# The last FFN block's down-projection as seven block products, and the delayed norm's stores issued one step later

## The chip, the cores and the metric

The kernel runs on one core of a Trainium2 chip. The metric is the device time of one execution in microseconds (us), the median of repeated runs. In this text PE is TensorE's matmul, PEld its weight load, DVE is VectorE, ACT is ScalarE, POOL is GpSimd, and SP is SyncE, whose queue (SPq in the profile) issues the DMAs this text is about.

## The reference, cut to what matters

One layer of a hybrid encoder: RMSNorm, a combined projection, chunk-band attention beside an mLSTM, an output projection, and then a gated convolutional feed-forward network. The change touches only the last part:

```python
def conv_ffn(h, buf, w_up, w_conv, b_conv, w_down):
    u = h @ w_up
    ext = jnp.concatenate([buf.astype(u.dtype), u], axis=1)
    y = b_conv
    for j in range(CONV_W):
        y = y + ext[:, j:j + S] * w_conv[j]
    gate, up = jnp.split(y, 2, axis=-1)
    out = (jax.nn.gelu(gate, approximate=True) * up) @ w_down
    return out, ext[:, S:]
...
    ffn, new_buf = conv_ffn(rms_norm(x, norm_g[2]), conv_buf, w_up, w_conv, b_conv, w_down)
    x = x + rms_norm(ffn, norm_g[3])
```

D_MODEL is 1024, D_FF is 2816, and there are 2048 prompt tokens and 8 x 16 sample tokens, so 17 token tiles of 128. `@ w_down` has 2816 = 22 x 128 rows of contraction and 1024 = 2 x 512 output columns. All is float32.

## The kernel before, in words

**Precision.** Each float32 operand is split into a high part (ACT casts it to the matmul's format) and a low part (DVE subtracts the high part); a product is three matmuls, hi·hi, hi·lo and lo·hi (`mm3`, lines 95 to 97). So every weight block of 128 x 512 costs one ACT cast (line 1259) and one DVE subtraction (line 1260) before PE may use it, and every piece of the gated activations costs the same.

**The feed-forward part** works on three blocks of token tiles, `FBLOCKS`: block 0 has tiles 0 to 5, block 1 has tiles 6 to 11, and block 2, the last, has tiles 12 to 15 and the sample tile 16, which is five tiles. For each block an *up* phase runs over 22 values of f: seven block products instead of eight (Strassen-Winograd; P1 to P7), the convolution on DVE, ACT and POOL, the gate (`gt`), and a store of it to DRAM. Then comes the *down* phase, which loads the gated activations back and multiplies them by `w_down`.

**Down, plain form (blocks 0 and 2 before).** Two halves of the output columns (`dh`), and in each 22 steps k; a step is 3 matmuls of 512 columns for each token tile. Weight blocks come four at a time (`load_w`, tiles `wdr` from DRAM, `wdh`/`wdl` after the split, two buffers of four blocks), activations one k at a time (`fetch`, line 1510, tiles `gr`; `gh`/`gl` after the split). In block 0, `load_down` also forms sums of weight blocks and stores them to `wtd`, for later use. In block 2's second half (`tail`), the last six k are done tile by tile, and after each tile `finish` does its norm at once: the sum of squares on ACT, the reciprocal root on POOL (lines 78 and 84), two scalings on DVE (line 1410), the additions of x on POOL and DVE (line 1412), two stores (line 1413).

**Down, seven products (block 1 before).** The up phase stores, besides the gated activations, four sums of their blocks (`gs`, line 1611) to `gsd`. The two halves of the token tiles and the two halves of k form a 2 x 2 block product, done as seven products D1, D6, D2, D7, D5, D4, D3. Each has six *units* u: two k each, the last one k. A unit of three tiles is 768 columns (`fetch_unit`, line 1534, tiles `gq`). Each product needs its own 11 weight blocks, from `w_down` or from the sums in `wtd`. When a product ends, its three accumulators are copied or added on (`x2`, `x3`).

**The delayed norm.** Blocks 0 and 1 don't finish their tiles at once. They store both halves of the result to DRAM (`f0d`, `f1d`), and the next block's down phase does the rest of them, as units of the pipe `ahead`, one step after each k or unit: `later` (line 1415) loads the half row `f` and the half of `x` (lines 1419 and 1420), and a step later scales on DVE (line 1422), adds x on POOL (line 1423), and stores on SP (line 1424). That is 12 such half rows for each of blocks 1 and 2.

**What sets the order.** Each engine has a queue worked in order. A scheduler orders the program's instructions by a modelled timeline, except where `keep_in_program_order` fixes one. Almost all DMAs of this part go through SP's queue: one that waits for its data (a store) or for its buffer (a load) holds back all behind it. A DMA also waits for the one eight places before it to land. Buffers: 11 of 128 x 512 (`quad`: raw weights, half rows, x), 4 wide rows (`row`: `gq`, `gr`), 2 + 2 of split weights, 4 of split activations.

## Time and profile before

| | |
|---|---|
| three runs | 2792.59, 2793.82 (median), 2799.96 us |
| the profiled execution | 2789.77 us; its span 2787.7 us |
| block 1: up, and down | about 1850 to 2167 us, and 2167 to 2340 us of the span |
| block 2: up, and down | about 2350 to 2621 us, and 2621 to 2780 us |
| after the last matmul | 2780 to 2787.7 us |

Times in the profile are microseconds from the start of the span. A table of windows has a row for each stretch: its length, the busy time of each engine with the number of instructions in brackets, the clock that PE was granted (1.00 is full), the mean busy share of the 16 DMA engines, and the rate that they moved. A row of a timeline has the start, the length, the engine and line, the operation with the tile that it writes and those that it reads, and in square brackets the idle time before it with what ended that. A wait "<- POOL f L1423" ended with that instruction. Matmuls overlap, so the length of one (some 0.4 us at 512 columns) is not the distance between two.

### The profile page before, as it was taken

To read this page: it belongs to the slowest core of one execution; us is meant where nothing else is said; L and a number is where in the kernel's file an instruction comes from. 1 tells how busy PE (TensorE), PEld (TensorE's weight loads), DVE (VectorE), ACT (ScalarE), POOL (GpSimd) and SP (SyncE) were. 2 spreads that over 40 slices of the span, in tenths; PEclk is the share of its full clock that TensorE was granted. 3 is DMA by queue.
4 is the path that set the end of the run, shared out by engine and by line. 5 is a ranking of instruction groups with operands and counts; after the bars stand their busy time and mean duration, and the time that the engine had idled before them with its cause. 6 is when DMAs were issued, how large, how long until landed. Compare 5 with 4: busy or idle time off the path is not lost.

```text
span 2787.7 us, 47226 instructions
## 1 busy us (share of the span) xinstructions
PE 2711.9 (97%) x16488; PEld 2539.5 (91%) x16488; DVE 1939.6 (70%) x3562; ACT 1421.7 (51%) x2871; POOL 447.3 (16%) x876
## 2 busy tenths in 40 slices
PE   8999999999999999999999999999999899999998
PEld 7899999998899998878999998799999778999987
DVE  5344455655456668756999988658888786888865
ACT  4355455644356666533554455445445565555543
POOL 1000010212000002334211211111111221222221
PEclk9999999999999999999999999999999999999999
DMA  5544355456555455355655449855554797555585
GB/s 185 155 122 133 103 175 162 159 160 213 158 173 147 141 172 182 113 167 176 217 172 176 162 161 324 297 180 167 174 179 165 244 345 230 170 180 179 177 323 192
DMA packets 334316, 516.33 MB, mean 185 GB/s; under 512 B 57122, under 2 KB 162558, under 8 KB 333950
## 3 DMA queue, kind: packets, MB, share of 16 engines
q1 hardware_dynamic: 295486, 479.49, 53.4%
q10 hardware_dynamic: 38592, 33.83, 3.6%
q8 instruction: 129, 2.11, 0.3%
q14 instruction: 109, 0.89, 0.1%
HBM read 371.61 MB, written 144.72 MB: 185 GB/s over the span
## 4 chain that ended last, share of the span: by engine, by line
PE 51%; DVE 4%; DMA 3%; issue 1%; POOL 1%; ACT 1%; SPq 0%; DVEq 0%; POOLq 0%; ACTq 0%
PE uec L95 6%; PE uec L97 6%; PE uec L96 6%; PE dn L97 3%; PE dn L95 3%; PE dn L96 3%; PE ua L97 3%; PE ua L96 3%; PE ua L95 3%; PE dnm L97 2%; PE dnm L95 2%; PE dnm L96 2%; PE wo L95 2%; PE wo L96 2%; PE wo L97 2%; PE ub L96 1%
## 5 line engine op out<-in xcount | busy, mean ns | idle before, releaser
L95 PE MATMUL uec<-B,wuh 128*128 128x384 f32 (+1 forms) x720 | 234.5, 328 | 3.3 <-DVE uu L1466 2.5
L96 PE MATMUL uec<-B,wuh 128*128 128x384 f32 (+1 forms) x720 | 235.1, 327 | 0.0
L97 PE MATMUL uec<-B,wul 128*128 128x384 f32 (+1 forms) x720 | 234.2, 327 | 0.0
L1259 ACT CAST wuh<-wu 128x512 fp32r<-128x512 f32 x255 | 141.7, 617 | 114.5 <-PE uec L96 103.8
L95 PE MATMUL dn<-wdh,gh 128*128 128x512 f32 x444 | 175.1, 394 | 6.1 <-ACT gh L1259 3.4
L96 PE MATMUL dn<-wdl,gh 128*128 128x512 f32 x444 | 175.7, 396 | 0.0
L1260 DVE TENSOR_TENSOR wul<-wu,wuh 128x512 fp32r<-128x512 f32 x255 | 165.3, 684 | 3.5 <-DMA x2d<-mx 3.5
L97 PE MATMUL dn<-wdh,gl 128*128 128x512 f32 x444 | 165.2, 398 | 0.8 <-DVE gl L1260 0.8
L395 DVE CUSTOM_DVE_ANT_0 tmp<-s,nb 128x640 f32<-128x640 f32 (+4 forms) x128 | 94.4, 738 | 96.8 <-PE s L385 95.5
L95 PE MATMUL vo<-wi_h,hT 128*128 128x256 f32 x544 | 155.9, 287 | 0.6 <-DVE mt L201 0.6
L97 PE MATMUL vo<-wi_h,hT 128*128 128x256 f32 x544 | 156.3, 287 | 0.0
L96 PE MATMUL vo<-wi_l,hT 128*128 128x256 f32 x544 | 155.5, 286 | 0.0
L95 PEld LDWEIGHTS uec<-B,wuh 128*128 128x128 f32 x720 | 134.9, 188 | 5.3 <-DVE uu L1466 3.5
L95 PE MATMUL qk<-hT,wi_h 128*128 128x384 f32 (+1 forms) x384 | 129.7, 338 | 7.2 <-ACT qk_st L226 5.9
L96 PEld LDWEIGHTS uec<-B,wuh 128*128 128x128 f32 x720 | 135.3, 188 | 0.2
L97 PEld LDWEIGHTS uec<-B,wul 128*128 128x128 f32 x720 | 135.1, 188 | 0.0
L408 DVE TENSOR_TENSOR ptl<-pt,pth 128x640 fp32r<-128x640 f32 (+4 forms) x128 | 93.7, 738 | 57.4 <-ACT pth L407 56.3
L396 ACT ACTIVATE tmp<-tmp,mn 128x640 f32<-128x640 f32 (+4 forms) x128 | 97.6, 762 | 64.8 <-DVE mn L395 62.2
L1259 ACT CAST gh<-gr 128x768 fp32r<-128x768 f32 (+3 forms) x92 | 65.2, 719 | 128.0 <-PE dn L96 112.7
L96 PE MATMUL qk<-hT,wi_h 128*128 128x384 f32 (+1 forms) x384 | 128.8, 335 | 0.0
L97 PE MATMUL qk<-hT,wi_l 128*128 128x384 f32 (+1 forms) x384 | 128.6, 335 | 0.0
L96 PE MATMUL qb<-hT,wi_h 128*128 128x384 f32 (+1 forms) x384 | 127.8, 333 | 0.0
(440 smaller groups left out, 8998.5 us busy)
## 6 DMA issues: line engine op xcount, KB each, us to landing
wu<-in_w_up SPq DMA_DIRECT2D x220, 256.0 KB, 3.6
wu<-wsd SPq DMA_DIRECT2D x176, 256.0 KB, 3.7
wdr<-in_w_down SPq DMA_DIRECT2D x121, 256.0 KB, 5.7
wi_raw<-in_w_in SPq DMA_DIRECT2D x52, 512.0 KB, 4.0
wsd<-ws SPq DMA_DIRECT2D x88, 256.0 KB, 3.0
gr<-gd SPq DMA_DIRECT2D x39, 384.0 KB, 4.2
kraw<-kTd SPq DMA_DIRECT2D x112, 128.0 KB, 3.1
gr<-gd SPq DMA_DIRECT2D x39, 320.0 KB, 4.1
```

Of the source, the lines that this page charges most:

```text
L95: nc.tensor.matmul(out, ah, bh, start=start, stop=False, skip_group_check=onto)
L96: nc.tensor.matmul(out, ah, bl, start=False, stop=False, skip_group_check=onto)
L97: nc.tensor.matmul(out, al, bh, start=False, stop=stop, skip_group_check=onto)
L395: nc.vector.tensor_tensor_reduce(o_, s_, b_, 1.0, 3e38, ALU.add, ALU.min, accum_out=mn)
L396: nc.scalar.activation(tmp[:, :n], tmp[:, :n], AF.Exp, bias=mn, scale=-1.0, accum_out=rsum[:, i % 4, hh:hh + 1])
L408: nc.vector.tensor_tensor(s.ptl[:, sl, qc], ptv, s.pth[:, sl, qc], op=ALU.subtract)
L1259: nc.scalar.copy(h, r)
L1260: nc.vector.tensor_tensor(l, r, h, op=ALU.subtract)
```

## The change

The last block's down phase now takes block 1's form. Its tiles 12 and 13 (two tiles) and 15 and 16 (two tiles) form the two halves of the tokens. Tile 14, the fifth, rides along: its part for the first column half is computed within D1 and D2, which take three tiles, and for the second within D3 and a new product D0, which has one tile. The order is D1, D6, D2, D7, D5, D4, D0, D3. That is (3·3 + 4·2 + 1)·11·3 = 594 matmuls of 512 columns, where 2·22·5·3 = 660 were, and 8·11 = 88 weight blocks, where 2·22 = 44 were. The block's up phase forms and stores the sums, of 256 columns here, with seven stores for two f in place of two. `finish_now` finishes tiles 15 and 16 after D4; tiles 12 to 14 are finished at the end, after the last two units of D3, which are done tile by tile (nine matmuls each). The accumulator that was squared straight from PSUM for each tile is so only for tile 14; tiles 12 and 13 have an addition (line 1709) first. In `later` the store moves one step on, and is held in program order. Block 0 and the plain code change only in names; `gd` is shared since only block 0 uses it.

```diff
-    D1, D6, D2, D7, D5, D4, D3 = range(7)
+    D1, D6, D2, D7, D5, D4, D3, D0 = range(8)
...
+    D_ORDER = [None, [D1, D6, D2, D7, D5, D4, D3], [D1, D6, D2, D7, D5, D4, D0, D3]]
...
             nc.vector.scalar_tensor_tensor(v, v, rs, g3[:, c:c + 512], op0=ALU.mult, op1=ALU.mult)
             nc.gpsimd.tensor_tensor(v, v, x, op=ALU.add)
-            nc.sync.dma_start(out_rows(t)[:, c:c + 512], v)
             yield 0.0, 1.0
+            tc.keep_in_program_order(nc.sync.dma_start(out_rows(t)[:, c:c + 512], v))
+            yield 0.0, 0.0
...
-        plain = b != 1
+        plain = b == 0
...
+        def width(p):
+            return 384 if not last or p in (D1, D2, D3) else P if p == D0 else 256
...
+            if last:
+                nc.sync.dma_start(to(1, 384), gt[:, 0:384])
+                nc.sync.dma_start(to(2), half(gt, 1))
+                nc.sync.dma_start(to(6, 384)[:, 256:384], gt[:, 256:384])
...
+        def finish_now(j, lo, hi):
+            t = tiles[j]
+            for c, v in ((0, lo), (512, hi)):
+                x = quad(f"x{t}_{c}")
+                nc.sync.dma_start(x, x2d[t][:, c:c + 512])
+                nc.vector.scalar_tensor_tensor(v, v, res[j], g3[:, c:c + 512], op0=ALU.mult, op1=ALU.mult)
+                nc.gpsimd.tensor_tensor(v, v, x, op=ALU.add)
+                nc.sync.dma_start(out_rows(t)[:, c:c + 512], v)
...
+                if last and q == len(units) - 2:
+                    rests = [load_rest(b, j) for j in range(2)]
+                    continue
+                if last and q == len(units) - 1:
+                    for j in range(3):
+                        for k in range(3):
+                            multiply(q - 1 + k // 2, j, k % 2)
+                        ssq = p3.tile([P, 1], F32, tag=f"dssq{j}", name=f"dssq{tiles[j]}_1", bufs=2)
+                        hi = x2[:, j]
+                        o = acc[j]
+                        if j < 2:
+                            o = hi
+                            nc.vector.tensor_tensor(o, o, acc[j], op=ALU.add)
+                        nc.scalar.activation(junk, o, AF.Square, accum_out=ssq)
+                        finish(b, j, rests[j], hi, o, ssq, res[j])
```

SP's queue in block 1's down phase, at the delayed norm's first two stores. `f` and `x` are the half rows, `gq` a unit of activations, `wdr` a raw weight block. Before:

```order
L1419 DMA f_24938<-f1d_194 128x512
L1420 DMA x_24939<-x2d_327 128x512
L1534 DMA gq_9_24979<-gsd_3_279 128x768
L1424 DMA out_y_prompt<-f_24917 128x512
L1424 DMA out_y_prompt<-f_24938 128x512
L1534 DMA gq_10_25017<-gsd_4_280 128x768
L1313 DMA wdr_4_0_24959<-wtd_314 128x512
L1313 DMA wdr_4_1_24963<-wtd_315 128x512
```

The same place now:

```order
L1419 DMA f_24899<-f1d_194 128x512
L1420 DMA x_24900<-x2d_288 128x512
L1540 DMA gq_9_24939<-gsd_3_240 128x768
L1425 DMA out_y_prompt<-f_24878 128x512
L1540 DMA gq_10_24977<-gsd_4_241 128x768
L1313 DMA wdr_4_0_24919<-wtd_275 128x512
L1313 DMA wdr_4_1_24923<-wtd_276 128x512
L1313 DMA wdr_4_2_24927<-wtd_277 128x512
```

The second store has moved behind the next unit and the next four weight blocks; the first stands where it stood.

SP's queue in the last block around the new product D0, whose weights are `wdr_18` to `wdr_20`; `wdr_21` is D3's first, `gq_41` and `gq_42` are units of D0 and D3, and line 1663 is `finish_now`'s store, which waits for POOL. There is no such place in before; now it reads:

```order
L1313 DMA wdr_20_0_31124<-in_w_down 128x512
L1663 DMA out_y_prompt<-c_2_0_31044 128x512
L1313 DMA wdr_20_1_31128<-in_w_down 128x512
L1540 DMA gq_41_31140<-gsd_5_248 128x128
L1663 DMA out_y_prompt<-dx_1_29957 128x512
L1313 DMA wdr_20_2_31132<-in_w_down 128x512
L1663 DMA out_y_sample<-c_2_1_31062 128x512
L1540 DMA gq_42_31152<-gsd_0_243 128x768
L1313 DMA wdr_21_0_31162<-in_w_down 128x512
L1663 DMA out_y_sample<-dx_1_29957 128x512
L1313 DMA wdr_21_1_31166<-in_w_down 128x512
```

The weights of D0's last unit and of D3's first stand between and behind four stores.

DVE's queue at the program's end. `f` is the first column half of a tile and `fr` or `dx` the second; `n_12_rs` and so on is the tile's reciprocal root. Before, its last eight rows:

```order
L1410 SCALAR_TENSOR_TENSOR fr_1_31099<-dn_1_0_30561,n_14_rs,norm_row_16271 128x512
L1412 TENSOR_TENSOR fr_1_31099<-fr_1_31099,xb_31095 128x512
L1410 SCALAR_TENSOR_TENSOR f_31130<-f_31130,n_15_rs,norm_row_16271 128x512
L1410 SCALAR_TENSOR_TENSOR fr_1_31099<-dn_1_1_30562,n_15_rs,norm_row_16271 128x512
L1412 TENSOR_TENSOR fr_1_31099<-fr_1_31099,xb_31132 128x512
L1410 SCALAR_TENSOR_TENSOR f_31166<-f_31166,n_16_rs,norm_row_16271 128x512
L1410 SCALAR_TENSOR_TENSOR fr_1_31172<-dn_1_0_30561,n_16_rs,norm_row_16271 128x512
L1412 TENSOR_TENSOR fr_1_31172<-fr_1_31172,xb_31168 128x512
```

And now (line 1709 adds a tile's last accumulator):

```order
L1709 TENSOR_TENSOR dx_0_29956<-dx_0_29956,dn_0_29954 128x512
L1410 SCALAR_TENSOR_TENSOR f_31329<-f_31329,n_12_rs,norm_row_16232 128x512
L1410 SCALAR_TENSOR_TENSOR dx_0_29956<-dx_0_29956,n_12_rs,norm_row_16232 128x512
L1709 TENSOR_TENSOR dx_0_29956<-dx_0_29956,dn_0_29954 128x512
L1412 TENSOR_TENSOR dx_0_29956<-dx_0_29956,xb_31331 128x512
L1410 SCALAR_TENSOR_TENSOR f_31335<-f_31335,n_13_rs,norm_row_16232 128x512
L1410 SCALAR_TENSOR_TENSOR dx_0_29956<-dx_0_29956,n_13_rs,norm_row_16232 128x512
L1410 SCALAR_TENSOR_TENSOR f_31367<-f_31367,n_14_rs,norm_row_16232 128x512
L1410 SCALAR_TENSOR_TENSOR dx_0_29956<-dn_1_29955,n_14_rs,norm_row_16232 128x512
L1412 TENSOR_TENSOR dx_0_29956<-dx_0_29956,xb_31337 128x512
L1412 TENSOR_TENSOR dx_0_29956<-dx_0_29956,xb_31369 128x512
```

After the second addition of line 1709, which waits for the program's last nine matmuls, seven rows follow, where three followed before.

174 lines of the change are left out of this document (85 added, 89 removed).

## The prediction, made before the run

> **What bounds the kernel now.** First the page: how busy each engine is, and which engine the chain that ended last runs through.
>
> ```profile
> span 2787.7 us, 47226 instructions
> PE 2711.9 (97%) x16488; PEld 2539.5 (91%) x16488; DVE 1939.6 (70%) x3562; ACT 1421.7 (51%) x2871; POOL 447.3 (16%) x876
> PE 51%; DVE 4%; DMA 3%; issue 1%; POOL 1%; ACT 1%; SPq 0%; DVEq 0%; POOLq 0%; ACTq 0%
> ```
>
> PE is busy 97% of the span, and its line on the chain is the longest, so a matmul less shows in the time wherever PE doesn't wait. An average hides where it does. So next, the table of windows over the stages that the change touches: block 0's up phase (two rows), block 2's up phase, block 1's down phase (two rows), block 2's down phase (two rows).
>
> ```profile
> core 0: us, PE busy (x) PEld busy (x) DVE busy (x) ACT busy (x) POOL busy (x), PEclk, DMA share, GB/s
> 1350.00:1650.00 300.00, 296.99 (x1697) 294.72 (x1696) 277.77 (x427) 152.86 (x245) 57.82 (x81) 1.00 0.52 174
> 1600.00:1650.00 50.00, 48.27 (x276) 47.63 (x275) 44.32 (x68) 25.62 (x41) 8.59 (x14) 1.00 0.54 180
> 2350.00:2621.00 271.00, 271.00 (x1845) 270.47 (x1844) 233.04 (x474) 152.90 (x269) 60.70 (x175) 1.00 0.55 175
> 2200.00:2260.00 60.00, 52.65 (x234) 39.84 (x232) 51.63 (x68) 38.99 (x68) 19.46 (x15) 1.00 0.87 291
> 2260.00:2310.00 50.00, 49.74 (x217) 39.91 (x218) 39.28 (x61) 29.14 (x58) 6.63 (x8) 1.00 0.99 350
> 2640.00:2690.00 50.00, 50.00 (x219) 40.85 (x218) 32.08 (x39) 18.16 (x28) 18.18 (x11) 1.00 1.03 379
> 2700.00:2750.00 50.00, 50.00 (x219) 40.93 (x218) 25.63 (x38) 23.39 (x43) 1.10 (x5) 1.00 0.73 248
> ```
>
> Block 2's up and down phases lose nothing inside. Block 1's down phase, the form that block 2 is to take, lost 60 − 52.65 = 7.35 us in 60. And the DMA engines are full (share about 1) at 350 to 379 GB/s.
>
> **Term 1, the matmuls: −15.1 us.** 660 − 594 = 66 matmuls go. In the row 2700:2750 PE never waits and does 219 in 50 us, 0.228 us each. 66 x 0.228 = 15.1.
>
> **Term 2, block 2's up phase: +2.5.** Added are 4 sums for each of 11 pairs of f, 44 DVE instructions of 256 columns. Rows of both neighbouring widths:
>
> ```profile
> L1611 DVE TENSOR_TENSOR gs<-g 128x384 f32<-128x384 f32 x10 | 5.5, 554 | 0.1
> L1466 DVE TENSOR_TENSOR uu<-x,uec 128x128 f32<-128x128 f32 x44 | 12.4, 281 | 7.9 <-PE uec L97 7.9
> ```
>
> Midway is 0.42 us, 18.4 us in all. DVE then has 233.0 + 18.4 = 251.4 us of 271, or 93%. Block 0's up phase ran at 277.77/300 = 93% and PE lost 3.0 us in 300, which is 2.7 in 271. I take 2.5; the ends are 0 (block 2 now, at 86%) and 5. The five more stores for each pair wait in SP's queue for DVE as block 1's did, in an up phase in which SP has room.
>
> **Term 3, the start of down: +2.5.** PE waited 2.10 us there in block 2 and 3.04 in block 1:
>
> ```profile
> 2631.00 0.64 PE L95 MATMUL dn<-wdh,gh 128*128 128x512 f32 x1 [2.10 <-DVE ug L1466]
> 2191.15 0.79 PE L95 MATMUL dn<-wdh,gh 128*128 128x512 f32 x1 [3.04 <-ACT gh L1259]
> ```
>
> With seven products DVE has to end the gate of f = 21 and its sums before it splits the fifth unit of activations, and D1 has 9 matmuls for a weight block where 15 were, 2.05 us where 3.42 were. So I expect two or three waits of one to two microseconds (second weight group, fifth and sixth unit, D6's first weights) in place of one: +2.5, ends 0 and 5.
>
> **Term 4, DMA from the delayed norm's start to D3: +10.5.** In the new order of SP's queue, 155 DMAs stand from the norm's first load to D3's first weights: 70 weight blocks (18.4 MB), 38 units (9.2), 24 loads and 12 stores of the norm (9.4), 3 stores of D2's result, and `finish_now`'s 4 loads and 4 stores (2.9): 39.9 MB. PE's work in that time is 423 matmuls (27 left of D1, then 66, 99, 66, 66, 66, 33), x 0.228 = 96.6 us. That asks for 413 GB/s. At the rate of 2640:2690, a mix of weights, activations and the same norm, 39.9 MB take 39.9/0.379 = 105.3 us, 8.7 more than PE needs; at 2260:2310's 350 GB/s they take 114.0, 17.4 more. I take the first, whose mix is the nearer, and keep the second as an end.
>
> The Trainium skill, "DMA: Bandwidth & Descriptors", section Specifications, puts a core's share of HBM at about 358 GB/s, and says that this binds transfers between HBM and SBUF. By that page of the Trainium skill 39.9 MB would take 111.5 us, 14.9 more than PE's work, and the whole sum would be about +8. The trace disagrees with it here: 379 GB/s over 50 us in the row 2640:2690.
>
> The shortage gathers at D0. It does 33 matmuls (7.5 us), but needs 11 weight blocks like the others, and the order put its last two behind stores that wait for POOL. Rows for that chain:
>
> ```profile
> wdr<-in_w_down SPq DMA_DIRECT2D x18, 256.0 KB, 6.3
> L1675 DVE TENSOR_TENSOR dx<-dx,dn 128x512 f32<-128x512 f32 x2 | 1.3, 680 | 0.0
> L1622 ACT ACTIVATE junk<-c 128x512 f32<-128x512 f32 x3 | 1.9, 636 | 0.0
> L1422 DVE SCALAR_TENSOR_TENSOR f<-f,drs,norm_row 128x512 f32<-128x512 f32 x12 | 8.9, 745 | 3.3 <-DMA f<-f1d 2.8 <-DMA f<-f0d 0.5
> L1423 POOL TENSOR_TENSOR f<-f,x 128x512 f32<-128x512 f32 x12 | 21.0, 1753 | 47.1 <-DVE f L1422 26.2 <-DMA wdr<-wtd 10.0 <-DMA gq<-gsd 6.4
> L1259 ACT CAST wdh<-wdr 128x512 fp32r<-128x512 f32 x34 | 19.6, 617 | 7.4 <-DMA wdr<-in_w_down 7.3
> L1260 DVE TENSOR_TENSOR wdl<-wdr,wdh 128x512 fp32r<-128x512 f32 x34 | 23.9, 743 | 6.2 <-ACT wdh L1259 6.2
> ```
>
> Counted from D4's last matmul: addition 0.7, square 0.6 (and 0.2 to read it out), root on POOL about 0.8, scaling 0.7, POOL's addition 1.8: 4.8. D0's last block goes out after a second addition, 6.6, and lands 6.3 later, 12.9; with cast and subtraction it is 14.3. PE wanted it at about 6.8, so D0 alone waits 7.5, whatever the rate was before. Most of it is the same shortage (the queue holds 2.6 MB at D4's end, 6.9 us at 379 GB/s), so I don't add it: 8.7, and 1.8 for time in which SP waits for POOL and the DMA engines run dry. Ends: 6 (the chain alone, landing sooner) and 17.4.
>
> **Term 5, the end: +4.** The chain behind the last matmul before:
>
> ```profile
> 2779.77 0.40 PE L97 MATMUL dn<-wdh,gtail 128*128 128x512 f32 x1
> 2780.25 0.60 ACT L1389 ACTIVATE junk<-dn 128x512 f32<-128x512 f32 x1 [4.07 <-issue]
> 2780.75 0.19 ACT L1389 ACTIVATION_READ_ACCUMULATOR junk<-dn 128x1 f32 x1
> 2781.04 0.26 POOL L78 TENSOR_SCALAR n_ms<-dssq,dssq 128x1 f32<-128x1 f32 x1 [1.24 <-ACT junk L1389]
> 2781.39 0.55 POOL L84 TENSOR_TENSOR n_rs<-n_ms,nhalf 128x1 f32<-128x1 f32 x1
> 2781.97 0.75 DVE L1410 SCALAR_TENSOR_TENSOR f<-f,n_rs,norm_row 128x512 f32<-128x512 f32 x1 [1.62 <-POOL n_rs L84]
> 2782.64 0.74 DVE L1410 SCALAR_TENSOR_TENSOR fr<-dn,n_rs,norm_row 128x512 f32<-128x512 f32 x1
> 2783.42 1.20 DVE L1412 TENSOR_TENSOR fr<-fr,xb 128x512 f32<-128x512 f32 x1
> 2784.64 0.33 SPq L1413 DMA_DIRECT2D out_y_sample<-fr  x1
> ```
>
> From 2780.17 (PE's end) to 2784.62 (DVE's) are 4.45 us, and 3.1 more to the span's end. Now an addition stands ahead (0.7), and DVE has two tiles to end, not one: two more scalings (1.4) and one more addition (1.2). That is +3.3, and up to +4.6 where DVE gets to line 1709 only after the tile before's scalings. I take 4; ends 2 and 5.
>
> **Term 6, block 1's delayed norm: −2.5.** The second store's wait, and what it held back:
>
> ```profile
> 2199.62 3.88 SPq L1424 DMA_DIRECT2D out_y_prompt<-f  x2
> 2206.19 0.37 SPq L1534 DMA_DIRECT2D gq<-gsd  x1
> 2212.17 0.50 PE L95 MATMUL dnm<-wdh,gh 128*128 128x512 f32 x1 [1.56 <-ACT gh L1259]
> SPq L1424 <- POOL f L1423: 17.7, 10, 3.6
> ```
>
> The unit `gq` at 2206.19 stood behind the two stores; it landed late, and PE waited 1.56 us for its split. By the same reading, about 4.2 of the 7.35 us in 2200:2260 lie behind such stores. A store one step later finds POOL done. But the DMA engines are 87% busy there already, and the units and weights that no longer wait meet a full queue: I take 2.5 of 4.2, ends 0 and 4.2. In block 2 the same edit is inside term 4: no store of the norm holds the queue there, or it would be more.
>
> **The sum:** −15.1 + 2.5 + 2.5 + 10.5 + 4 − 2.5 = +1.9 us. The profiled execution took 2789.77 us (2.1 around its span), 4 below the median of 2793.82; the same difference on the median gives 2795.7. About 0.3% (8.4 us) is what a measurement of this kernel can tell from no change, so the likeliest result is that nothing can be told.
>
> **Rivals.**
>
> *The saving shows.* If the queue runs well ahead, so that D0's own chain is all that is left of term 4 (6.0), the start costs 0.5, up nothing, the end 3, and block 1 gains its whole 4.2, the sum is −15.1 + 0.5 + 6.0 + 3 − 4.2 = −9.8: 2784.0. For it: 2640:2690 kept PE full at 379 GB/s. Against it: there PE's own demand was far lower and the rest could come late.
>
> *Starved of weights: slower.* The place is D6 to D0. Term 4 with its 1.8 reaches 17, and the sum +8.4, when 39.9 MB take 96.6 + 15.2 = 111.8 us, at 357 GB/s; below that rate the change loses. At 350 GB/s term 4 is 19.2 and the sum +10.6: 2804.4. For it: 2260:2310 ran at 350 with the engines full. The ceiling of the Trainium skill's page that is cited in term 4 lies at this point. Against it: 379 over 50 us of nearly this mix.
>
> *The up phase becomes DVE's.* If all of block 2's up goes as 1600:1650 (1.73 us lost in 50), it loses 9.4 and the sum is +8.8: 2802.6. Against it: that is block 0's worst stretch.
>
> **Chances.** The forecast 0.60; the saving shows 0.18; starved 0.17; DVE's up phase 0.05. So faster by over 0.3% is 0.18, within 0.60, slower 0.22. The range reaches from the first rival to a little past the second, whose rate may fall further: 2784 to 2807, with the ends of terms 1 to 6 adding up to −11 and +17.
>
> **What would show it.** Right: the windows of block 2's up at 92 to 94% DVE and one to 5 us lost; a DMA share near 1.0 from about 2640 on for 100 us; PE's longest wait at D0 and at D3's first matmuls, for `gh` or `wdl` behind line 1313; 10 to 12 us from the last matmul to the span's end; waits of line 1425 on POOL in block 1 far under 17.7 us. Wrong: D6 to D0 in about 90 us (term 4 too large), or a DMA share well under 0.9 with PE waiting, which would mean that the order of SP's queue, not the rate, decides.

## The result, and the profile after

The changed kernel took 2808.29 us (median of 6, 2807.19 to 2811.78), the kernel before beside it 2792.30 (median of 6, 2786.47 to 2799.96): ratio 1.0058 with a 95% interval of [1.0042, 1.0073]. On another chip, beside the last experiment, it was 2809.27 against 2786.44: 1.0085 [1.0072, 1.0099]. So the change makes the kernel slower, by 0.6 to 0.9%; the forecast was 2795.7, the range ended at 2807.0. The profiled execution's span grew by 17.8 us, from 2787.7 to 2805.5.

First the lines of the page after, which answer to the three quoted of before: PE has 66 matmuls less and is busy 10.3 us less, in a span that is longer.

```profile
span 2805.5 us, 47483 instructions
PE 2701.6 (96%) x16422; PEld 2522.9 (90%) x16422; DVE 1981.2 (71%) x3655; ACT 1447.6 (52%) x2922; POOL 458.4 (16%) x878
PE 49%; DMA 5%; DVE 4%; issue 1%; ACT 1%; SPq 1%; POOL 0%; DVEq 0%; POOLq 0%; ACTq 0%
```

On the chain DMA has grown from 3% to 5%. The table of windows after: block 1's down, block 2's up, two stretches of block 2's down that the prediction used, ten and twenty microseconds around the new product D0, and the stretch from the norm's first load (2642.40) to D3's first matmul (2768.10).

```profile
core 0: us, PE busy (x) PEld busy (x) DVE busy (x) ACT busy (x) POOL busy (x), PEclk, DMA share, GB/s
2200.00:2260.00 60.00, 51.77 (x223) 40.50 (x222) 50.12 (x67) 36.82 (x65) 18.63 (x15) 0.97 0.85 283
2350.00:2621.00 271.00, 271.00 (x1843) 270.35 (x1842) 244.69 (x511) 153.76 (x267) 71.08 (x173) 1.00 0.63 196
2640.00:2690.00 50.00, 38.79 (x141) 28.64 (x140) 31.11 (x44) 19.65 (x32) 13.20 (x10) 0.90 1.02 365
2700.00:2750.00 50.00, 49.39 (x211) 39.04 (x209) 35.12 (x59) 33.95 (x67) 1.16 (x5) 1.00 0.77 267
2740.00:2750.00 10.00, 10.00 (x44) 7.87 (x42) 6.48 (x12) 6.05 (x12) 0.00 (x0) 1.00 0.17 52
2750.00:2770.00 20.00, 11.81 (x40) 8.12 (x40) 16.80 (x22) 10.05 (x21) 8.56 (x8) 0.83 0.94 322
2642.40:2768.10 125.70, 106.14 (x418) 81.44 (x416) 89.11 (x128) 66.84 (x125) 26.48 (x25) 0.93 0.91 322
```

Up loses nothing, with DVE at 244.69/271 = 90%. The loss is in down, at two places: 2640 to 2690 (PE busy for 38.79 of 50, with full DMA engines at 365 GB/s) and 2750 to 2770 (11.81 of 20). Between them the DMA engines nearly stood still, at 0.17. From its first matmul of 512 columns to the start of its last, block 2's down took 171.9 us (2620.44 to 2792.35), where before took 160.1 (2619.67 to 2779.77); this stretch, called *the phase* below, grew by 11.8, and what follows it, to the span's end, by 5.2 (from 7.9 to 13.1).

PE's waits of over a microsecond in the phase, from the timeline (in brackets the wait, and what ended it):

```profile
2651.09 0.50 PE L95 MATMUL dnm<-wdh,gh 128*128 128x512 f32 x1 [3.44 <-ACT wdh L1259]
...
2659.79 0.50 PE L95 MATMUL dnm<-wdh,gh 128*128 128x512 f32 x1 [1.07 <-ACT wdh L1259]
...
2669.86 0.80 PE L95 MATMUL dnm<-wdh,gh 128*128 128x512 f32 x1 [3.85 <-ACT wdh L1259]
...
2678.14 0.50 PE L95 MATMUL dn<-wdh,gh 128*128 128x512 f32 x1 [1.21 <-ACT wdh L1259]
2680.28 0.50 PE L96 MATMUL dn<-wdl,gh 128*128 128x512 f32 x1 [1.41 <-DVE wdl L1260]
...
2751.74 0.47 PE L95 MATMUL dn<-wdh,gh 128*128 128x512 f32 x1 [1.65 <-DVE c L1741]
...
2758.92 0.80 PE L95 MATMUL dn<-wdh,gh 128*128 128x512 f32 x1 [4.16 <-ACT wdh L1259]
2761.28 0.79 PE L96 MATMUL dn<-wdl,gh 128*128 128x512 f32 x1 [1.57 <-DVE wdl L1260]
```

All but one end with the split of a weight block: weights come late, first at D6 and D2 (the first five), just after the delayed norm has begun, and again in D0 (the last three; the first of these ends with DVE's copy of D4's accumulators). SP's queue says why they are late (its own timeline; "x4" are four issues in a row):

```profile
2639.36 0.33 SPq L1617 DMA_DIRECT2D gsd<-g  x1
...
2642.40 0.40 SPq L1419 DMA_DIRECT2D f<-f0d  x1
...
2644.77 1.94 SPq L1313 DMA_DIRECT2D wdr<-wtd  x4
...
2734.82 15.04 SPq L1540 DMA_DIRECT2D gq<-gsd  x7
2749.91 1.85 SPq L1660 DMA_DIRECT2D x<-x2d  x4
2751.81 2.54 SPq L1313 DMA_DIRECT2D wdr<-in_w_down  x5
```

D6's first weights are issued at 2644.77, behind the stores of the last gate (line 1617, from 2639.36) and four loads of the norm, and PE wants them at 2647.6. (What stands ahead of a late load need not be the cause: without the norm's loads PE waits as long about here, as e3_no_norm shows below.) D0's second group is issued at 2751.81, behind seven unit loads that took 15 us, each waiting for a row buffer that DVE has to free, and behind `finish_now`'s four loads of x.

### The profile page after: what moved, and what is told of

It is laid out like the page before. It is cut to its first block, busy times and chain, and to the rows that moved or that the text cites. A ratio compares the mean times of both kernels' runs of the same rounds, so it can differ in the third digit from the quotient of the medians.

```text
span 2805.5 us, 47483 instructions
## 1 busy us (share of the span) xinstructions
PE 2701.6 (96%) x16422; PEld 2522.9 (90%) x16422; DVE 1981.2 (71%) x3655; ACT 1447.6 (52%) x2922; POOL 458.4 (16%) x878
## 4 chain that ended last, share of the span: by engine, by line
PE 49%; DMA 5%; DVE 4%; issue 1%; ACT 1%; SPq 1%; POOL 0%; DVEq 0%; POOLq 0%; ACTq 0%
PE uec L95 6%; PE uec L96 6%; PE uec L97 6%; PE dn L96 3%; PE dn L97 3%; PE dn L95 3%; PE ua L97 3%; PE ua L96 3%; PE ua L95 3%; PE wo L95 2%; PE wo L97 2%; PE wo L96 2%; PE dnm L97 1%; PE ub L96 1%; PE ub L97 1%; PE ub L95 1%
## 5 line engine op out<-in xcount | busy, mean ns | idle before, releaser
L95 PE MATMUL dn<-wdh,gh 128*128 128x512 f32 x473 | 188.1, 398 | 11.7 <-ACT wdh L1259 5.8
L96 PE MATMUL dn<-wdl,gh 128*128 128x512 f32 x473 | 189.0, 400 | 3.3 <-DVE wdl L1260 3.3
L97 PE MATMUL dn<-wdh,gl 128*128 128x512 f32 x473 | 183.5, 402 | 0.5 <-DVE gl L1260 0.4
L1260 DVE TENSOR_TENSOR wdl<-wdr,wdh 128x512 fp32r<-128x512 f32 x209 | 137.7, 700 | 24.8 <-ACT wdh L1259 24.1
L1259 ACT CAST wdh<-wdr 128x512 fp32r<-128x512 f32 x209 | 120.2, 617 | 58.9 <-DMA wdr<-wtd 19.8
```

What stands on the lines that cost most here:

```text
L95: nc.tensor.matmul(out, ah, bh, start=start, stop=False, skip_group_check=onto)
L96: nc.tensor.matmul(out, ah, bl, start=False, stop=False, skip_group_check=onto)
L97: nc.tensor.matmul(out, al, bh, start=False, stop=stop, skip_group_check=onto)
L1259: nc.scalar.copy(h, r)
L1260: nc.vector.tensor_tensor(l, r, h, op=ALU.subtract)
```

## The experiments

"Changed" is the changed kernel. *Phase* is as above, read from each profile; the two profiles of the changed kernel had 171.9 and 174.8, so a few microseconds in it tell nothing. One profile is one execution: that of e15_tail took 2813.67 us, 5.5 above the kernel's median, that of e12_norm_up_all 2819.03, 6.7 above, that of e17_no_bytes 2796.06, 5.9 below. The chips differ too, hence ratios to before on the same chip.

| kernel | median us | ratio, 95% interval | phase us |
|---|---|---|---|
| before (first chip) | 2792.3 | 1 | 160.1 |
| changed | 2808.3 | 1.0058 [1.0042, 1.0073] | 171.9 |
| e18_changed_again | 2809.3 | 1.0085 [1.0072, 1.0099] | 174.8 |
| e1_old_store | 2813.3 | 1.0089 [1.0076, 1.0102] | 178.5 |
| e2_before_new_store | 2785.7 | 0.9996 [0.9985, 1.0007] | 160.2 |
| e3_no_norm | 2798.3 | 1.0032 [1.0019, 1.0044] | 162.4 |
| e4_d0_early | 2811.1 | 1.0078 [1.0063, 1.0092] | 174.0 |
| e5_spread | 2807.0 | 1.0070 [1.0055, 1.0085] | 171.8 |
| e6_d0_bank | 2807.9 | 1.0077 [1.0065, 1.0090] | 173.7 |
| e7_finish_late | 2805.2 | 1.0063 [1.0051, 1.0075] | 172.3 |
| e8_d0_mixed | 2815.1 | 1.0090 [1.0075, 1.0104] | 174.3 |
| e9_order | 2803.6 | 1.0053 [1.0040, 1.0066] | 171.2 |
| e10_late_norm | 2810.5 | 1.0080 [1.0067, 1.0094] | 175.8 |
| e11_norm_up | 2822.7 | 1.0124 [1.0109, 1.0139] | 161.1 |
| e12_norm_up_all | 2812.3 | 1.0080 [1.0066, 1.0094] | 156.0 |
| e13_own_rows | 2809.3 | 1.0087 [1.0074, 1.0100] | 170.3 |
| e14_own_all | 2800.8 | 1.0060 [1.0044, 1.0075] | 164.5 |
| e15_tail | 2808.2 | 1.0082 [1.0069, 1.0095] | 178.0 |
| e16_stalls (of before) | 2804.6 | 1.0067 [1.0055, 1.0078] | 179.0 |
| e17_no_bytes | 2802.0 | 1.0065 [1.0052, 1.0079] | 166.8 |

### The store that moved (term 6)

e1_old_store puts the store of `later` back into the changed kernel; e2_before_new_store moves it in before.

```diff
             nc.gpsimd.tensor_tensor(v, v, x, op=ALU.add)
+            nc.sync.dma_start(out_rows(t)[:, c:c + 512], v)
             yield 0.0, 1.0
-            tc.keep_in_program_order(nc.sync.dma_start(out_rows(t)[:, c:c + 512], v))
-            yield 0.0, 0.0
```

> The changed kernel with the delayed norm's store back in its old place, one step earlier, and nothing else undone. Term 6 as forecast (the move saves 2.5 us in block 1): undoing it costs 2.5, so about 2810.8 us where the changed kernel has 2808.3. What the trace of after suggests (block 1's windows 2180 to 2260 lost 1.6 us more than before, and the unit of activations behind the store was issued at 2213.0 with the old place and with the new, so the store held back nothing that mattered): undoing it is worth 0 to 1.6 us, 2806.7 to 2808.3. If the new place is what crowds the start of block 2's down phase: under 2804.

> The kernel before with only the store of the delayed norm moved one step later. Term 6 as forecast: 2.5 us less, about 2789.8 where before has 2792.3. By the trace of after: no gain, 2792.3 to 2794, with block 1's waits on POOL in SP's queue gone and PE's waits in 2195 to 2235 about as long as before.

Measured: for e2 0.9996, with an interval that holds both no gain and the forecast's 2.5 us; for e1 1.0089, where the changed kernel had 1.0058 and 1.0085. So the times can't tell, and the traces must. In block 1 the move gained nothing that lasted: block 2's down phase begins at 2620.3 us in e1, with the old store, and at 2620.4 in the changed kernel. SP's queue there, after, then before: the unit load that stood behind the second store, the next one, and the one after that.

```profile
2201.03 0.32 SPq L1540 DMA_DIRECT2D gq<-gsd  x1
...
2203.64 0.32 SPq L1540 DMA_DIRECT2D gq<-gsd  x1
...
2213.01 0.32 SPq L1540 DMA_DIRECT2D gq<-gsd  x1
```

```profile
2203.62 0.36 SPq L1534 DMA_DIRECT2D gq<-gsd  x1
...
2206.19 0.37 SPq L1534 DMA_DIRECT2D gq<-gsd  x1
...
2213.25 0.32 SPq L1534 DMA_DIRECT2D gq<-gsd  x1
```

With the store gone from ahead of them, two loads went 2.6 us earlier, and PE's wait of 1.56 us behind them (at 2212.17 in before) fell to 0.56 (at 2210.17). The third load went at the same time as before: it waits for one of four row buffers, which DVE's split of an older unit frees (from 2212.04 on in after). PE then waited 1.67 us, at 2213.04. One stop of the queue hid the next. In block 2 e1's profile has a longer phase, 178.5, and its median is 4 to 5 us above the changed kernel's; whether the old store costs something there stays open.

### The norm in block 2's down phase (term 4, first place)

e3_no_norm leaves the last block's norm out (the rows of tiles 6 to 11 stay unwritten); e5_spread and e10_late_norm only move it (e10 on top of e9 and e6, below); e11_norm_up does it in block 2's up phase; e13_own_rows gives it buffers that no weights use; e17_no_bytes keeps its arithmetic but loads once and stores once (those rows are not right).

```diff
-        ahead = Pipe(iter(done) if last else h2_units(b + 1, done))
+        ahead = Pipe(iter([]) if last else h2_units(b + 1, done))                        # e3
+        ahead = Pipe(iter([x for u in done for x in (u, bubble(), bubble())]) if last    # e5
...
-            v, x, c = quad(f"f{half}{t}"), quad(f"x{half}{t}"), half * 512
+                own = (ffn.p3 if i < EARLY_B else ffn.p4).tile([P, 3072], F32, tag=f"B{i}", name=f"own{half}{t}", bufs=1)   # e13
+                v, x = own[:, 0:512], own[:, 512:1024]
...
+                v, x = kept[0]                                                           # e17
```

> The changed kernel without the delayed norm of block 1's tiles in the last block: 24 loads, 12 stores, 12 scalings and 12 additions are left out, so the rows of tiles 6 to 11 are not written. Theory A (the norm's 9.4 MB crowd D6's and D2's weights): the 11 us of waits between D1 and D2 and some 4 of slow clock behind them go, D0's wait stays: about 2794. Rival O (D6's weights come late because their DMAs stand behind the store of the last gate, f = 21, whatever the norm does): the first wait of 3.4 us stays with its slow clock: about 2800. If the weights alone are too much for the DMA engines: over 2804. The DMA share between 2645 and 2690 should fall from 1.03 to about 0.75 under A and O.

> The changed kernel with the last block's delayed norm spread out: a half row every third unit instead of every unit, so it lies beside D1 to D5 instead of D1 to D2. From the run without the norm (9.5 us less from block 2's first down matmul to its last: 162.4 us against 171.9), theory burst (the norm's 9.4 MB are too dense beside D6 and D2): spread, most of the 9.5 comes back, phase 163 to 165 us, ratio to before about 1.003. Theory total (the down phase as a whole asks for about what the DMA engines give, so bytes moved later are missed later): the loss moves to D7, D5 and D0, phase 169 to 172, ratio 1.005 to 1.006. Slower than the changed kernel if half rows held longer take the raw weights' buffers.

> The kernel of e9_order, with tile 14's second half in the bank of its first, and the last block's delayed norm from unit 8 on (D6's third) with a half row every second unit, so that D6's first weights no longer stand behind four loads of the norm. Theory order: the wait of 3.4 us at D6's first matmul falls below 1.5, the three that follow (6.5 us together) to 3, D0's to 2: down phase 160 to 163 us, ratio 0.999 to 1.002. Theory total (the phase asks for what the DMA engines give at most): the waits move to D7, D5 and D4, phase 167 or more, ratio 1.004 or more.

> The changed kernel with the delayed norm of block 1's tiles done in block 2's up phase (12 half rows over 18 values of f), where the DMA engines are busy for 0.64, instead of in its down phase. Down phase as in the run without the norm: 162 to 163 us where 172 was. The price is in up: DVE at 93% takes 12 more scalings of 0.75, 9 us, and two raw buffers of 11 are held by a half row; if DVE bounds up, it loses 5 or more of the 9.5 gained (ratio 1.004), if not, ratio 1.002 to 1.003.

> The changed kernel with the last block's delayed norm in buffers of its own (those of the up phase's normed inputs, which are free by then) instead of the 11 that hold raw weights; loads, bytes and arithmetic are the same. Theory buffers: D6's and D2's weights go ahead in SP's queue, the four waits of 2651 to 2680 (9.8 us) fall to 3 or less, and the down phase comes to 162 to 165 us, as without the norm, ratio about 1.003. Theory rate: the bytes are the same, the waits stay within 2 us of 9.8, phase 170 to 173, ratio 1.005 to 1.007.

> The changed kernel in which the last block's delayed norm loads one half row and one half of x in place of twelve each, does all twelve scalings and additions on them, and stores once: 22 loads and 11 stores, 8.7 MB, are left out, and so the right rows of tiles 6 to 11. Theory bytes: the phase falls as without the norm, to 162 to 165 us from 172. Rival engines (DVE's splits are held up by the scalings, and run at half speed beside POOL's additions): the phase stays at 168 or more. Rival buffers is part of theory bytes here, since two raw buffers are held instead of up to six; e13_own_rows put that part at 1.6 us.

Without the norm the phase is 9.5 us shorter than the first profile of the changed kernel (12.4 than the second). The time, 2798.3, lies between theory A's 2794 and rival O's 2800, nearer O. Three lines of e3's timeline, and one of e12_norm_up_all (below), which does the norm in up:

```profile
2646.11 0.50 PE L95 MATMUL dn<-wdh,gh 128*128 128x512 f32 x1 [4.55 <-ACT gh L1259]
...
2749.78 0.80 PE L95 MATMUL dn<-wdh,gh 128*128 128x512 f32 x1 [3.90 <-ACT wdh L1259]
2752.41 0.79 PE L96 MATMUL dn<-wdl,gh 128*128 128x512 f32 x1 [1.83 <-DVE wdl L1260]
```

```profile
2673.06 0.50 PE L95 MATMUL dn<-wdh,gh 128*128 128x512 f32 x1 [4.74 <-ACT gh L1259]
```

The four waits from 2659 to 2681 in after (7.5 us together) are gone, and with them the slow matmuls behind the second of them: that is the norm's price. The first wait is not gone. It is 4.55 us in e3, 4.10 in e11 and 4.74 in e12, where no load of the norm stands in the phase, and it ends there with the cast of a unit of activations, 768 columns wide, so one of D1's. In e3 the queue took seven loads of weights ahead of that unit's load (from 2633.81 us on, where the norm's and the last gate's DMAs stood ahead of D6's weights in after), and the weights were in time. So O was right that the wait stays, though another load is the late one now, and the norm's loads are not its cause. D0's waits stay too (7.3 us with 1.57 at 2742.86), while the DMA engines were busy for 0.66 of 2645 to 2690: they are no part of the norm's crowd.

Spread or later, the norm costs the same. In e5 the waits at D6 and D2 fall from 11.0 to 5.6, and those from D4 to D3 grow (9.1 where 8.2 were). In e10 the first wait is still there (4.57 at 2642.57, again for a unit of D1), and others have come in the second half of the phase (1.72, 2.09, 1.65, 1.02 and 2.68); the DMA engines have 0.78 in the first half and 0.86 in the second. Burst is out; what theory total forecast came. Own buffers (e13) let the weights go ahead in SP's queue, and then units of activations were late instead (a third wait for one, 3.00 us, at 2675.44):

```profile
2646.56 0.79 PE L95 MATMUL dn<-wdh,gh 128*128 128x512 f32 x1 [3.81 <-ACT gh L1259]
...
2663.37 0.50 PE L97 MATMUL dnm<-wdh,gl 128*128 128x512 f32 x1 [1.24 <-DVE gl L1260]
```

Its ratio is that of the changed kernel: the buffers are not the cause. With the bytes out and the arithmetic kept (e17) the phase is 166.8, 5.1 or 8.0 less than in the two profiles of the changed kernel and 4.4 more than in e3; neither theory's range (162 to 165, or 168 and more) was met. So the norm's price seems to be in part its bytes and in part its work on DVE and POOL, but these differences are hardly larger than that of two profiles of one kernel, and the shares can't be told. The whole phase in one row each, for before, after, e3_no_norm and e17_no_bytes:

```profile
2619.70:2780.20 160.50, 158.08 (x685) 128.51 (x684) 97.69 (x136) 64.26 (x112) 32.18 (x33) 0.99 0.73 255
```

```profile
2620.30:2792.60 172.30, 151.73 (x621) 118.09 (x619) 121.58 (x184) 88.84 (x162) 31.37 (x33) 0.95 0.82 290
```

```profile
2620.60:2783.40 162.80, 148.83 (x623) 116.87 (x622) 108.38 (x173) 87.25 (x163) 15.66 (x22) 0.97 0.75 249
```

```profile
2613.90:2781.20 167.30, 150.49 (x620) 116.88 (x619) 124.48 (x184) 87.24 (x162) 34.41 (x33) 0.96 0.72 246
```

Share times length is the work of the DMA engines: before 0.73 x 160.5 = 117 us, beside 150 us of down matmuls (660 x 0.228). After it is 0.82 x 172.3 = 141 us, beside 594 x 0.228 = 135. The change took the matmuls below the transfers, so less time is left in which a stop of the queue can hide. But the transfers' sum alone doesn't set the length: without the norm they have 122 us, in e17 120, in e12 also 120, all less than the matmuls, and these phases are 162.4, 166.8 and 156.0 long. So something else counts too: the queue's order does, as e12 shows; DVE's work may. No run made DVE's splits cheaper (its busy time in the phase grew from 97.69 to 121.58 us), so its part isn't separated.

In up (e11) the norm costs more than it saves in down: the phase is 161.1, about as forecast, but it starts 25.4 us later (2645.9 against 2620.4).

```profile
2400.00:2600.00 200.00, 183.93 (x1219) 181.13 (x1218) 177.86 (x357) 102.01 (x176) 70.63 (x127) 0.98 0.70 214
```

```profile
DVE f L1422 <- DMA f<-f1d: 13.9, 5, 4.3
```

DVE is not full there (178 of 200): it waits, in order, for the norm's loads (13.9 us in that stretch for `f1d` alone), and up's own work stands behind. The expected reason, DVE's load, doesn't fit: it is busier in up of the changed kernel (186.60 of the same 200 us) without a wait of PE.

### D0 (term 4, second place)

e4_d0_early puts D0 between D7 and D5. e6_d0_bank lets it use another PSUM bank. e7_finish_late does tiles 15 and 16 step by step, from D0's fifth unit on. e8_d0_mixed alternates its groups with D3's. e9_order is e7 with D0's and D3's first weights and units held in program order.

```diff
-    D_ORDER = [None, [D1, D6, D2, D7, D5, D4, D3], [D1, D6, D2, D7, D5, D4, D0, D3]]
+    D_ORDER = [None, [D1, D6, D2, D7, D5, D4, D3], [D1, D6, D2, D7, D0, D5, D4, D3]]                      # e4
...
-                    acc = acc[:2] + [banks[1 if p in (D3, D0) else 0][2]]
+                    acc = acc[:2] + [banks[0][2]]                                  # e6
...
-                            finish_now(j + 3, o, x3[:, j])
+                            late_.extend(finish_late(j + 3, o, x3[:, j]))          # e7
...
+        return g_ if b == 1 or not g_ else g_[:18] + [(D0, 0), (D3, 0), (D0, 1), (D3, 1), (D0, 2), (D3, 2)]   # e8
...
+            if nm in ("2_18", "2_19", "2_20", "2_21"):
+                tc.keep_in_program_order(load)                                     # e9
```

> The changed kernel with D0 between D7 and D5, so that it no longer stands beside the finishing of tiles 15 and 16. Theory chain (D0's last weights and D3's first wait in SP's queue behind the stores that wait for POOL, and DVE does the finishing ahead of D0's splits): the 8 us of waits at 2752 to 2769 and the 2.7 of slow clock go, less what D3's start still waits: about 2799. Rival weights (D0 asks for 11 blocks, 2.9 MB, in 7.5 us, which at 379 GB/s take 7.6 us on top of its units): it loses about as much at its new place: 2806 to 2809.

> The changed kernel with tile 14's second column half summed in the PSUM bank that its first half used (free after D2) instead of the bank beside an accumulator of D4. Theory: PE's wait of 1.65 us at D0's first matmul, ended by DVE's copy of D4's accumulator, is there only since the two lie in one PSUM tile; the wait goes. If D0's weights are the real limit, the waits for them (4.16 and 1.57 us) grow by as much and the time stays: ratio 1.0058. If not: 1.6 us less, ratio 1.0052, which is less than the runs can tell, so the trace decides: the waits between D4's last matmul and D3's, 8.2 us in after, become 6.5 or stay 8.2.

> The changed kernel with the finishing of tiles 15 and 16 (4 loads of x, 4 scalings, 4 additions, 4 stores) done step by step beside D0's end and D3, instead of at D4's end. Term 4's chain (D0's last weights stand in SP's queue behind stores that wait for POOL, and the splits in DVE's queue behind scalings): the 4.16 and 1.57 us of waits for D0's weights go, 5 to 7 us less, ratio about 1.0035. Rival (moving D0 away from the finishing cost 8.7 us of waits at its new place, so D0's waits are from its own 11 weight blocks in 7.5 us of matmuls): at most 2 us less, ratio 1.005 to 1.006.

> The changed kernel with D0's three weight groups placed between D3's (D0, D3, D0, D3, D0, D3), so that 4 blocks of weights are asked for in 2.7 us only ahead of a group of D3 that takes 8.2. Theory weights (D0 starves since it asks for 2.9 MB of weights and 0.7 of units in 7.5 us): the waits of 5.7 us for D0's weights fall to 2 or less, ratio about 1.004, unless D3's last units then come late. Theory chain (the finishing of tiles 15 and 16 holds the queues): the first D0 group still waits for the copy of D4's accumulators, and the first D3 group waits as long as D0 did: ratio 1.006.

> The kernel of e7_finish_late, and in SP's queue D0's and D3's first weights and units in the order in which the program writes them. In after, seven loads of units stood in SP's queue from 2734.8 to 2749.9, each until DVE had split an older unit, with D0's second group of weights behind them, while the DMA engines were busy for 0.17 of 2740 to 2750. Theory order (D0's weights come late because they stand behind unit loads that wait for a row buffer): PE's waits from D4's last matmul to D3's second group, 8.2 us in after and 4.7 in e7_finish_late, fall to 2 or less, and the down phase to 168 us from 172. Theory rate: they stay at 4 or more, since the DMA engines can't bring 11 blocks in the time.

D0 early: PE waited 2.05, 2.57 and 1.36 us in it at its new place, and 2.75 at D3, 8.7 in all: as much as before, so theory chain is not all. Mixed with D3's groups its first group waited as before (1.65), and D3's first group behind it waited as D0's second had (3.94 and 2.42), which is what theory chain said of it. With the other bank the 1.65 went, the waits for weights stayed (5.21 and 0.66 in place of 4.16 and 1.57), and 6.7 of 8.2 were left. With the finishing moved away, the waits from D4 to D3's start are 4.1 us, half of after's 8.2 (20 − 11.81 in the table):

```profile
2755.35 0.47 PE L95 MATMUL dn<-wdh,gh 128*128 128x512 f32 x1 [1.31 <-DVE c L1752]
...
2760.55 0.50 PE L97 MATMUL dn<-wdh,gl 128*128 128x512 f32 x1 [1.16 <-DVE gl L1260]
...
2768.61 0.50 PE L95 MATMUL dn<-wdh,gh 128*128 128x512 f32 x1 [1.63 <-ACT gh L1259]
```

So of D0's 8.2 us about 4 come from the finishing, 1.3 to 1.6 from the bank, by one profile each. In program order (e9) the queue no longer stops (DMA share 0.80 in 2740 to 2750, where it was 0.17), and yet 4.2 us of waits stay in 2750 to 2770, where 2 were expected: theory order fails on size. DVE is busy there for 9.07 of the first ten; D0's 11 weight blocks at 0.62 us and six units at about 0.4 are some 9 us of splits beside 7.5 us of matmuls. With the bank's edit as well, in e12 and e14 below, 2.3 us of D0's waits are left. e9's interval, which ends at 1.0066, is the only one of the five that lies wholly below that of e18_changed_again, and it still holds the first measurement's 1.0058; e9 has e7's edit too.

### Do the causes add up? And a faster version?

e12_norm_up_all is e11 with e6, e7 and e9; e14_own_all is e13 with e6, e7, e9 and e15.

> The kernel of e11_norm_up with the late finishing of tiles 15 and 16, the order of D0's weights, and tile 14's second half in the bank of its first. If the three causes (norm beside D6 and D2, SP's order at D0, the bank) add up, the down phase takes 153 to 156 us, and the kernel is about as fast as before or faster: ratio 0.996 to 1.000, less what up loses. If D0's waits are from the rate: phase 160 or more, ratio over 1.002.

> The kernel of e9_order (late finishing of tiles 15 and 16, D0's weights in program order) with the norm in buffers of its own, tile 14's second half in the bank of its first, and the last three tiles in the order 14, 12, 13. If the causes add up as in e12_norm_up_all, whose down phase took 156.0 us: phase 156 to 159, the stretch from the last matmul to the span's end 10 to 11 us in place of 13, so ratio 0.999 to 1.001. If the bytes are the cause: phase 168 or more, ratio 1.004 or more.

```profile
2647.80:2804.20 156.40, 146.32 (x621) 115.48 (x619) 105.29 (x172) 86.39 (x162) 13.75 (x20) 0.99 0.77 257
```

That is e12's phase: 156.0 us, at the end of what was expected, 4.1 less than before's, with the clock back at 0.99. So the norm and D0's queueing account for the phase's loss, and the eight products can be the shorter down phase. The time is not shorter: up lost 27 us for it. e14, which keeps the norm in down, has 164.5 where 156 to 159 was expected, or 168 and more: it still does the norm's 9.4 MB, and it waits 1.61 and 3.00 us for splits of units at 2661.88 and 2673.96, where e12 has no such wait. (Both have the first wait, before D6: 4.30 and 4.74 us.) Its end takes 13.6 us where 10 to 11 was expected, and its ratio is 1.0060. No version here is faster than before: even e12's 4.1 us are less than the 5.2 that the end costs.

### The end (term 5)

e15_tail does the last three tiles in the order 14, 12, 13, so that the tile without an addition comes first.

```diff
-                    for j in range(3):
+                    for j in (2, 0, 1):
```

> The changed kernel with the last three tiles done in the order 14, 12, 13 instead of 12, 13, 14. Theory: at the end DVE's queue holds two tiles to scale and add behind the last addition (line 1709), since tile 14's comes last there though its matmuls were done earlier; with 14 first only one tile and the addition are left: from the last matmul to the span's end 10 to 11 us where after has 12.9. Rival: the last chain is one tile's own (addition, square, root, scalings, addition, store), whatever the order: 12.5 to 13. Ratio 1.005 or 1.006.

From the last matmul's start to the span's end: 13.2 us, as in after (13.1). That is the rival's forecast of no change (12.5 to 13), not the 10 to 11 of the theory. DVE's queue of after, then of e15, from the addition of line 1709 that waits for the last matmuls:

```profile
2793.46 0.68 DVE L1709 TENSOR_TENSOR dx<-dx,dn 128x512 f32<-128x512 f32 x1
...
2797.36 1.75 DVE L1410 SCALAR_TENSOR_TENSOR f<-f,n_rs,norm_row 128x512 f32<-128x512 f32 x1
...
2799.69 1.91 DVE L1412 TENSOR_TENSOR dx<-dx,xb 128x512 f32<-128x512 f32 x2
```

```profile
2803.11 0.68 DVE L1709 TENSOR_TENSOR dx<-dx,dn 128x512 f32<-128x512 f32 x1
```

In e15 the addition came at 2803.11, over four microseconds after its matmuls (they ended at about 2799), behind the scalings and an addition of tiles 14 and 12: the same work in another order. And the scaling that took 1.75 us began during an addition on POOL (2797.16 to 2798.56); the others took 0.75. The 1.91 us are two additions, of 1.31 and 0.68.

### What a wait of PE costs beyond itself

e16_stalls puts five waits into before's block 2 down, by copying raw activations onto themselves on ACT.

```diff
+                for _ in range({(0, 8): 6, (0, 12): 8, (0, 16): 10, (1, 4): 12, (1, 8): 9}.get((dh, k), 0) if last else 0):
+                    nc.scalar.copy(r[:, :nt * P], r[:, :nt * P])
                 split(gh, gl, r[:, :nt * P])
```

> The kernel before with five waits put into block 2's down phase: at five of its 44 steps the raw activations are copied onto themselves 6 to 12 times on ACT ahead of their cast, so PE has to wait for them (the result is the same). Theory clock: behind each wait of more than two microseconds some 8 to 11 matmuls run at 0.43 instead of 0.23 us apart, so the phase grows by the idle time that the trace shows and 1.5 to 2.3 us more for each such wait. Rival: the slow matmuls in after come from the busy DMA engines or from the change's smaller groups, and the phase grows by the idle time alone (within 1 us in all).

Three of the five came out as waits of over a microsecond (2.95, 4.12 and 4.53 us). The phase grew by 18.9 us (160.1 to 179.0), PE's idle time in it by 12.7 (2.4 to 15.1). So 6.2 us came on top, behind these three. PE's timeline behind the last of them:

```profile
2729.27 0.66 PE L95 MATMUL dnm<-wdh,gh 128*128 128x512 f32 x1 [4.53 <-ACT gh L1259]
...
2730.15 0.63 PE L95 MATMUL dnm<-wdh,gh 128*128 128x512 f32 x1
...
2732.29 0.63 PE L96 MATMUL dn<-wdl,gh 128*128 128x512 f32 x1
...
2733.72 0.39 PE L95 MATMUL dn<-wdh,gh 128*128 128x512 f32 x1
2733.95 0.39 PE L96 MATMUL dn<-wdl,gh 128*128 128x512 f32 x1
```

Matmuls start 0.43 us apart (2730.15 to 2732.29, five steps, of which the lines show the ends) for some 4 us, then 0.23 apart again. In 2730 to 2740 the granted clock is 0.86. Theory clock holds: the groups here are before's, and the DMA engines are at 0.49 in these ten microseconds.

### The changed kernel again

> The changed kernel itself, beside the others on this chip. If the chips differ in nothing that matters: ratio 1.0058 as before, within 1.0042 to 1.0073, down phase 170 to 174 us. If single executions of the same program vary as the runs with small edits did (171 to 178 us in this phase), the phase is up to 6 us off and the ratio up to 1.008.

2809.27 us, 1.0085: the changed kernel's own time is that of the first measurement, the kernel before was 6 us faster on this chip. The waits lie at the same places (3.98 at D6, 3.35 and 2.66 in D0).

## Why the prediction was wrong

The signs of terms 1, 3, 4 and 5 were right, and the sum failed on the size of term 4.

- **Term 1 (−15.1): right.** 66 matmuls went, and where PE doesn't wait it still does one in 0.228 us (44 in the 10.00 us of 2740:2750).
- **Term 2 (+2.5): nothing lost.** DVE came to 90% in the whole stretch, and to 186.60 of 200 in 2400 to 2600, without a wait of PE. So DVE's share alone was not what block 0 lost its time to; no run here shows that cause. Inside the ends that were given.
- **Term 3 (+2.5, ends 0 and 5): about +1.5.** Before the norm's first load PE waited for nothing, where before had 2.10 us and eight slow matmuls behind it (1.6): −3.7. D6's first weights, which the term named, were late by 3.44, and nine slow matmuls behind them cost 1.8 (estimate: 9 x 0.20, from the timeline). The norm's loads stood ahead of these weights, but without them PE waits no less (4.55 in e3_no_norm, for D1's fifth unit, which the term named too), so it belongs here.
- **Term 4 (+10.5, ends 6 and 17.4): the step that failed.** The bytes were right: 125.7 us at 322 GB/s are 40.5 MB, forecast 39.9. So was the work: 418 matmuls, forecast 423, 95.3 us. But the stretch took 125.7 us, 30.4 more than its matmuls, of which 19.6 are idle time (125.70 − 106.14) and 10.8 slow matmuls; without the 5.2 that belong to term 3, 25.2 are left. The sentence that failed is "Most of it is the same shortage, so I don't add it": the prediction took one shortage of transfers, at 379 GB/s, for the whole stretch. The runs show two losses that stand apart. Without the norm the later waits at D6 and D2 go and D0's 7.3 us stay, although the DMA engines have room; with the finishing moved (e7) half of D0's waits go and those at D6 and D2 stay. Nor was the rate the right measure: it came from a stretch where the queue never stopped (2640:2690 of before) and was used for a queue with new stops in it, above all the ten microseconds at 0.17 before D0. At the full engines' 365 GB/s of 2640:2690 the 40.5 MB take 111 us, 15.7 more than the matmuls. If they were the loss, e17, which moves 8.7 MB less (31.8 MB are 87 us at this rate, less than the matmuls), should have lost them all, and its phase lost 5.1 to 8.0; how much of term 4 is rate isn't shown. The rival of the starved weights put its limit at 357 GB/s. The mean was below it, though the engines ran at 365 to 399 where they were full, so its mechanism isn't what the trace shows. It was the nearest of the four, with a price of 10.6 where the profile has 17.8, and that is in part luck.
- **What no term had:** the slow clock behind each wait. PE's busy time in the stretch of term 4 is 10.8 us longer than its matmuls need; by the granted clock's mean of 0.93 up to 8.8 of them (0.07 x 125.7) can be the clock, and the rest isn't explained. The Trainium skill, "TensorE: Matmul & The Clock Gate", Part 1, says that after an idle window of some 3.4 us the clock halves, for about 3.4 us. The trace agrees on half speed and on the length (0.43 against 0.23 us, some 4 us long). It differs on the idle time: in e5_spread a wait of 2.06 us at 2670.37 was followed by such a stretch, though in e4_d0_early one of 2.05 at 2725.70 was not.

```profile
2670.37 0.50 PE L96 MATMUL dn<-wdl,gh 128*128 128x512 f32 x1 [2.06 <-DVE wdl L1260]
...
2671.81 0.63 PE L96 MATMUL dnm<-wdl,gh 128*128 128x512 f32 x1
2672.24 0.63 PE L97 MATMUL dnm<-wdh,gl 128*128 128x512 f32 x1
```

- **Term 5 (+4, ends 2 and 5): +5.2.** The chain was as described, and DVE reached line 1709 only after tile 12's scalings. From PE's end to DVE's were 8.85 us (2792.75 to 2801.60), 4.4 more than before, as forecast for that case (up to 4.6), with one scaling at 1.75 us and not 0.75. The other 0.8 came behind DVE: 3.9 us to the span's end, where before had 3.1. The Trainium skill, "SBUF — State Buffer", section "SBUF: two separate sides", says that VectorE and GpSimd share a pair of ports under an exclusive lock. The trace agrees: the scaling of 1.75 us began during POOL's addition and ended 0.55 us behind it.
- **Term 6 (−2.5): nothing that can be told.** "About 4.2 of the 7.35 us lie behind such stores" read a wait by what stood ahead in the queue, not by what would stop it next.

The sum of what the profile has: −15.1, 0, +1.5, +25.2, +5.2, 0, and 0.8 by which block 2's down started later: 17.6; the span's growth is 17.8.

Of the signs named for right, PE's longest wait in D0 came; DVE's 92 to 94% in up (90), a DMA share near 1.0 for 100 us (0.77 in 2700 to 2750) and 10 to 12 us at the end (13.1) did not, and line 1425 still waited 11.5 us for POOL in block 1, where 17.7 had been. Of those named for wrong, one came: a DMA share well under 0.9 ahead of a wait of PE (0.17 in 2740 to 2750), the order of SP's queue. What stays open: how the norm's price splits between its bytes and its work on DVE and POOL; and what would remove the four microseconds of wait between D1 and D6, which came whichever load went first. That e15, which differs only in its last tiles, has 178.0 us in this phase, 6 more, fits its profiled execution, which took 5.5 us more than its median.

## What to carry to other kernels

Compare the work of the DMA engines (share times length) with that of PE in the stretch that is cut: when matmuls are saved by more weight loads, the transfers can become the longer of the two. Here spreading the late loads or giving them buffers then moved the loss and didn't remove it. Don't fold two waits into one shortage because they stand in the same stretch: leave each one's work out in turn and see whether the other stays. Take the rate from a stretch with the new queue's stops or leave room for them, and add about two microseconds to most waits of PE of over two for the clock behind them. Before a wait in a queue is booked as a gain, or put down to what stands ahead of it, look for the next wait behind it.

## What the runs showed of the hardware that was not expected

Nearly every wait of PE of two to five microseconds was followed by 7 to 13 matmuls at half speed (0.43 us apart instead of 0.23), which cost some 1.5 to 2.7 us each: 6.2 us for three such waits in e16_stalls. The DMA engines moved 365 GB/s over 50 us (share 1.02 in 2640 to 2690 of after), and 399 in 2670 to 2680 (1.04). A scaling of 512 columns on DVE took 0.75 us alone and 1.75 where it began during an addition on POOL. PE's wait of 1.65 us for DVE's copy of D4's accumulators, before D0's first matmul, was gone when D0 summed in another PSUM bank (e6_d0_bank).
